# Hybrid RWKV-7 / RG-LRU / MLA layers in float32: the second pair's recurrences issued behind the state chain, another filling for TensorE inside it

## The chip, the cores and the metric

One Trainium2 chip, one NeuronCore. The metric is the device time of one execution in microseconds (us), the median of three runs of one program. The kernel is one launch with no collectives; its inputs lie in the chip's HBM, laid out on the host beforehand.

## The reference

Two layers over 512 tokens of width 1024, then a final RMS norm. Each layer norms `h`, multiplies it with `w_in` and cuts the product into three mixers, gates each by a silu, and adds `y @ w_out` to `h`:

```python
S = S * w_t[:, :, None, :] - sa[..., None] * b_t[:, :, None, :] + v_t[..., None] * k_t[:, :, None, :]   # RWKV-7, 8 heads of 64
...
xc = conv_b + sum(up[:, j:j + T] * conv_w[j] for j in range(CONV_W))        # RG-LRU, width 512, in 8 blocks of 64
gate_r = jax.nn.sigmoid(xb @ ga_w + ga_b); gate_i = jax.nn.sigmoid(xb @ gx_w + gx_b)
log_a = -LRU_C * gate_r * jax.nn.softplus(-lam); a = jnp.exp(log_a)
bx = jnp.sqrt(-jnp.expm1(2.0 * log_a)) * (gate_i * xc)
h_t = a_t * h_(t-1) + bx_t
...
q = rms_norm(q_lat) @ w_uq; kv = rms_norm(kv_lat) @ w_ukv                    # MLA, causal softmax, 8 heads
...
y = jnp.concatenate([y_a * silu(z_a), y_b * silu(z_b), y_c * silu(z_c)], -1); h = h + y @ w_out[l]
```

## The kernel before

All matrix products are float32 made of three float32r products: each operand is split into a high part H and a low part L (`split`, L209; `weights`, L217), and `mm3` (L232) adds H·H, H·L and L·H in PSUM. A piece of weights is loaded by a DMA of the SP queue into one of three `wr` buffers, ScalarE (ACT) copies its H, and VectorE (DVE) or GpSimd (POOL) subtracts to give L; the counter `wmod` says that every so many pieces go to DVE, the others to POOL.

The work of one layer is written as steps of a letter and a number, in the three strings ORD1 to ORD3 (L61 to L63), run in that order. The program's scheduler then places the instructions on each engine by readiness under its own estimate, keeping the priority of the program's order; on the chip each engine runs its list strictly in order and waits for semaphores. So what stands in front of what in an engine's list is fixed at build time.

The prediction is about ORD3, the stretch around the RWKV state chain, which each layer has once:

- **H0 to H7** (`chunk`, L841) are the eight chunks of 64 tokens. Each is a chain across two engines: sixteen small products of the state (L849, "u" below), two DVE additions into `UV` (L852), sixteen small products (L859, "so"), then two DVE instructions that give the next state: the sum with the old state into `S` (L863) and the product with the decays `PC` (L864). Every second chunk also forms the outputs (L877 from the states, L883 from `UV`, then L885 to L887). All `u` and `so` products use the two banks `ck` in turn.
- **A2, A3** (`lru_a`, L672): for one block of 128 channels the projection (24 TensorE matmuls), two ACT copies (L677, L679), three DVE instructions of the convolution (L681), eight small gate matmuls into two `ps` banks (L687), two sigmoids, a POOL product (L691), a tanh (L693).
- **B0, B1** (`lru_b`, L697): the recurrences of a pair of blocks: exp on ACT, the square on POOL (L702), two DVE instructions (L704, L705), a square root (L709) in another ACT table, a POOL product (L710), the DVE scan (L712), a square (L716, L718), a POOL sum (L719), a DVE product with the gate (L720).
- **g0, g1, g2, g3** (`gate`, L372): the four MLA gates, each a projection of 24 matmuls and a silu.
- **t0 to t7** (`lat_products`, L901): the latents' products, eight pieces of 12 matmuls with 416 columns into all four `acc` banks; **T0** copies the four banks out (L916, on ACT), **T1** norms them.
- **N** is the group norm of the chain's outputs (DVE), **R0** the token sums of the RG-LRU outputs (L379), **Y0** the splits of its outputs (L211).

The matmuls of A, g and t have no tie to the chain and fill TensorE (PE) while the chain is on DVE. There are two `ps` banks, four `acc` banks, three `wr` buffers and four each of `wH` and `wL`.

Of the kernel before, what the change touches and what calls it, by code (L numbers as in the profile page):

```python
# [1 line left out]

# [9 lines left out]
AF = mybir.ActivationFunctionType  # L12
# [4 lines left out]
T = 512  # L17
# [30 lines left out]
def body(ctx, tc, x, wc, wl, wo, w2a2, gagx, wuq, wukv, vec, ln_g, fin_g, cst, out, depth=DEPTH):  # L48
# [11 lines left out]
    BN = (2, 2, 0, 0)  # L60
    ORD1 = "M0 L0 L1 C0 M1 C1 P0 L2 O0 M2 U1 O1 C2 U2 P1 L3 M3 C3 U0 P2 O2"  # L61
    ORD2 = "G0 U3 G1 P3 G2 Z0 Z1 O3 G3 X0 f4 V0 V1 Z2 Q0 Q1 f0 V2 V3 f1 Q2 Q3 J0 f2 J1 K0 f3 W0 K1 W1 f5 W2 W3"
    ORD3 = "B0 H0 H1 A2 H2 H3 A3 H4 H5 H6 H7 B1 N0 g0 g1 t0 t6 t1 t2 t4 t5 t3 t7 T0 R0 Y0 g2 g3 T1"  # L63
    LO = "0ig12uw3yvcm"
    Q1 = "aoooottttaaaooookvvqvkqvkqkqqqqq"
    WA, WB, WC, WD, WF = 1000, 2, 2, 5, 1000

    def tl(tag, shape, dt=F32, bufs=1):
        cnt[0] += 1
# [2 lines left out]
    def g2(shape=(128, 512)):  # L72
        return tl("g2", shape, F32, bufs=11)
# [16 lines left out]
    def ps(shape=(128, 512)):  # L90
        cnt[0] += 1
        return PS.tile(list(shape), F32, tag="ps", name=f"ps_{cnt[0]}", bufs=2)
# [40 lines left out]
    def act(out, in_, func, **kw):  # L133
        st = {AF.Sigmoid: "S", AF.Tanh: "S", AF.Sqrt: "Q"}.get(func, "E")
        if cur[0] != st:
            chained(A.preload_act_table_set(SETS[st]))  # L136
            cur[0] = st
        chained(A.activation(out=out, in_=in_, func=func, **kw))  # L138

    def copy(out, in_, **kw):  # L140
        i = A.activation(out=out, in_=in_, func=AF.Copy, **kw)  # L141
        return getattr(i, "ins", i)
# [178 lines left out]
    def one_layer(l):  # L321
        def vc(n, j):
            o = VO[n] + j
            return vecs[:, l, o:o + 1]
# [6 lines left out]
        def proj(j, halves=False):  # L331

            if halves:
                o = acc()
                W = [weights(wc[l, j, :, 4 * hf:4 * hf + 4, :].rearrange("p k c -> p (k c)"), raw=raws.pop((j, hf), None)) for hf in range(2)]
                for th in range(2):
                    t = slice(th * 256, (th + 1) * 256)
                    for k in range(8):
                        s = slice((k % 4) * 128, (k % 4 + 1) * 128)
                        w = W[k // 4]  # L340
                        mm3(o[:, t], (w[0][:, s], w[1][:, s]), (xH[:, k, t], xL[:, k, t]), k == 0, k == 7)
                return o
            o, parts = proj_parts(j)
            for part in parts:
                part()
            return o
# [320 lines left out]
        gw = tl("w2", [128, 2, 4, 64])  # L667
        nc.sync.dma_start(out=gw, in_=gagx[l])

        st = {}  # L670

        def lru_a(*js, o=None):  # L672
            for j in js:
                o = o or proj(17 + j)
                ub = g2([128, T + 3])
                G.memset(ub[:, 0:3], 0.0)
                copy(ub[:, 3:], o)  # L677
                xc = g2()
                A.activation(out=xc, in_=o, func=AF.Identity, scale=vc("cw", 12 + j), bias=vc("cb", j))  # L679
                for t in range(3):  # L680
                    V.scalar_tensor_tensor(out=xc, in0=ub[:, t:t + T], scalar=vc("cw", 4 * t + j), in1=xc, op0=ALU.mult, op1=ALU.add)  # L681
                gt = []
                for w in range(2):
                    o = ps()
                    for e in range(2):
                        hr = slice(64 * e, 64 * e + 64)
                        PE.matmul(o[hr, :], gw[hr, w, j, :], xc[hr, :], start=True, stop=True)  # L687
                    s = g2()
                    act(s, o, AF.Sigmoid, bias=vc("gx_b" if w else "ga_b", j))
                    gt.append(s)  # L690
                G.tensor_tensor(out=gt[1], in0=gt[1], in1=xc, op=ALU.mult)  # L691
                th = g2()
                act(th, gt[0], AF.Tanh, scale=sp8[:, l, j:j + 1])  # L693
                st[j] = (gt[0], gt[1], th)
                o = None

        def lru_b(*js):  # L697
            for j in js:
                a, bx, th = st[j]
                act(a, a, AF.Exp, scale=nsp8[:, l, j:j + 1])  # L700
                a2 = g2()
                G.tensor_tensor(out=a2, in0=a, in1=a, op=ALU.mult)  # L702

                V.scalar_tensor_tensor(out=a2, in0=a2, scalar=1.0, in1=th, op0=ALU.add, op1=ALU.mult)  # L704
                V.tensor_scalar(out=a2, in0=a2, scalar1=1.0e-34, scalar2=None, op0=ALU.max)  # L705
                st[j] += (a2,)
            for j in js:
                a, bx, th, a2 = st[j]
                act(a2, a2, AF.Sqrt)  # L709
                G.tensor_tensor(out=bx, in0=bx, in1=a2, op=ALU.mult)  # L710
                hs = th
                V.tensor_tensor_scan(out=hs, data0=a, data1=bx, initial=0.0, op0=ALU.mult, op1=ALU.add)  # L712
                sq = a2
                if j == 0:
                    stb[0] = tl("sqn", [128, T])
                    A.activation(out=stb[0], in_=hs, func=AF.Square)  # L716
                else:
                    A.activation(out=sq, in_=hs, func=AF.Square)  # L718
                    G.tensor_tensor(out=stb[0], in0=stb[0], in1=sq, op=ALU.add)  # L719
                V.scalar_tensor_tensor(out=hs, in0=hs, scalar=vc("out_g", j), in1=gz[j], op0=ALU.mult, op1=ALU.mult)  # L720
                yb.append(hs)
# [119 lines left out]
        def chunk(ch):  # L841
            cp, par = ch // 2, ch % 2
            ur = slice(64 * (1 - par), 64 * (1 - par) + 64)
            if ch:
                uo = [ck([128, 4, 64]) for _ in range(2)]
                for p in range(4):
                    for e in range(2):
                        hr = slice(64 * e, 64 * e + 64)
                        PE.matmul(uo[e][ur, p, :], AR[p][hr, 0, ch * 64:(ch + 1) * 64], S[ch][hr, p, :], start=True, stop=True)  # L849
                for e in range(2):  # L850
                    u = UV[ur, :, ch, 64 * e:64 * e + 64]
                    V.tensor_tensor(out=u, in0=uo[e][ur, :, :], in1=u, op=ALU.add)  # L852
            if ch < 7:
                so = ck([128, 4, 64])
                for p in range(4):
                    for e in range(2):
                        hr = slice(64 * e, 64 * e + 64)
                        hc = slice(e * 64, (e + 1) * 64)
                        PE.matmul(so[hr, p, :], BT[p][:, ch, hc], UV[:, p, ch, hc], start=True, stop=True)  # L859
                sn = S[ch + 1] = tl("S", [128, 4, 64], bufs=3)  # L860
                pc = PC[:, :, ch:ch + 1].to_broadcast([128, 4, 64])
                if ch:
                    V.tensor_tensor(out=sn, in0=so, in1=S[ch], op=ALU.add)  # L863
                    V.tensor_tensor(out=sn, in0=sn, in1=pc, op=ALU.mult)  # L864
                else:
                    V.tensor_tensor(out=sn, in0=so, in1=pc, op=ALU.mult)
            if par == 0:
                return
            yt = c2([128, 4, 2, 64])
            sq = c2([128, 4, 2, 64])  # L870
            yo = [ps([128, 4, 64]) for _ in range(2)]

            for p in range(4):
                for e, q in ((0, 0), (1, 1), (0, 1), (1, 0)):
                    hr, uq, c = slice(64 * e, 64 * e + 64), slice(64 * q, 64 * q + 64), 2 * cp + q
                    if c:
                        PE.matmul(yo[e][uq, p, :], AR[p][hr, 1, c * 64:(c + 1) * 64], S[c][hr, p, :], start=p == 0, stop=False)  # L877
            for e in range(2):
                hc = slice(e * 64, (e + 1) * 64)
                for p in range(4):  # L880
                    for q in range(2):
                        uq, c = slice(64 * q, 64 * q + 64), 2 * cp + q
                        PE.matmul(yo[e][uq, p, :], AM[q][:, p * 8 + e * 4 + cp, 64:128], UV[:, p, c, hc], start=c == 0 and p == 0, stop=p == 3)  # L883
            for e in range(2):
                V.tensor_copy(out=yt[:, :, e, :], in_=yo[e])  # L885
                A.activation(out=sq[:, :, e, :], in_=yo[e], func=AF.Square)
            V.tensor_reduce(out=vr[:, cp, :, :], in_=sq, axis=AX.X, op=ALU.add)  # L887
            yts.append(yt)
# [53 lines left out]
        def b_split(_):  # L942
            yb[:] = [ysplit(y) for y in yb]

        steps.update({"H": chunk, "N": lambda _: group_norm(), "A": lru_a, "B": lambda i: lru_b(2 * i, 2 * i + 1), "R": b_sums, "Y": b_split,
                      "t": lat_products, "T": latents, "g": lambda p: gzc.append(gate(25 + p))})
        run(ORD2)
        run(ORD3)
# [278 lines left out]
```

## Time and profile before

| what | value |
|---|---|
| three runs | 848.09, 848.45, 851.1 us; median 848.45 |
| the profiled execution | 847.71 us, of which the span is 845.9 |
| mean granted TensorE clock | 0.984 |
| busy: DVE, ACT, POOL | 538.9, 519.3, 353.3 us |
| DMA | 91.07 MB, 108 GB/s on average |

The span is that of the recorded instructions. A row of the timeline gives the start in us from the span's start, the time from its first to its last end, engine, line, operation, output and inputs, the number of instructions merged, and in brackets the idle time before it and what ended it. Matmuls overlap, so their distance from start to start is the cost of one, not the duration in the row. The first layer's state chain stands at about 209 to 258 us of the span, the second layer's at 622 to 672.

### The profile page before, as it was taken

Reading aid. Unit: us, or ns where it says so; the run is one execution under the profiler, and the core shown is the slowest. Engines: PE = TensorE matmul, PEld = TensorE weight load, DVE = VectorE, ACT = ScalarE, POOL = GpSimd, SP = SyncE. Lnnn points to the kernel's source line nnn. Section 1 sums busy time; section 2 is a strip of 40 time slices with the busy share of each in tenths; the row PEclk is TensorE's granted clock in tenths of the full one; section 3 lists DMA queues with packets and bytes.
Section 4 is the critical chain, followed back from the end, with each engine's and each line's share of the span. In section 5 each row is a group of like instructions: output and inputs, shape, how many; then the busy total and the mean of one; then the engine's idle time right before and its main releaser. Section 6 shows DMA issues by size and latency. Waiting matters only on the chain. (4 is left out here: it accounts for less than half of the span.)

```text
span 845.9 us, 15219 instructions
## 1 busy us (share of the span) xinstructions
PE 791.7 (94%) x5696; PEld 619.4 (73%) x5696; DVE 538.9 (64%) x1115; ACT 519.3 (61%) x1018; POOL 353.3 (42%) x321
## 2 busy tenths in 40 slices
PE   4999999999879999999989999999998799999995
PEld 3878888886659877657778788888765697775674
DVE  5678776924977364774474966695367953577636
ACT  5667875657563576664467687845666436765635
POOL 0455557522452455022344556574143425530323
PEclk9999999999998999999999999999999899999998
DMA  7222134311113375123732233332001234731354
GB/s 246 98 76 74 66 111 132 112 58 33 33 39 113 120 229 193 55 90 92 272 122 89 75 100 100 101 112 92 30 26 43 80 95 140 244 120 50 112 174 162
DMA packets 49754, 91.07 MB, mean 108 GB/s; under 512 B 5520, under 2 KB 8336, under 8 KB 49680
## 3 DMA queue, kind: packets, MB, share of 16 engines
q1 hardware_dynamic: 49104, 89.05, 32.8%
q8 instruction: 45, 0.74, 0.4%
q10 hardware_dynamic: 576, 1.05, 0.3%
q14 instruction: 29, 0.24, 0.1%
HBM read 73.30 MB, written 16.78 MB: 106 GB/s over the span
## 5 line engine op out<-in xcount | busy, mean ns | idle before, releaser
L229 POOL TENSOR_TENSOR wL<-wr,wH 128x512 fp32r<-128x512 f32 (+1 forms) x148 | 196.8, 1336 | 283.9 <-ACT wH L141 270.4
L141 ACT ACTIVATE wH<-wr 128x512 fp32r<-128x512 f32 (+1 forms) x192 | 118.8, 622 | 142.8 <-PE acc L234 73.9
L233 PE MATMUL acc<-xH,wH 128*128 128x512 f32 (+1 forms) x496 | 191.9, 388 | 0.0
L234 PE MATMUL acc<-xL,wH 128*128 128x512 f32 (+1 forms) x496 | 189.3, 382 | 0.7 <-DVE xL L306 0.6
L235 PE MATMUL acc<-xH,wL 128*128 128x512 f32 (+1 forms) x496 | 188.5, 380 | 0.0
L234 PEld LDWEIGHTS acc<-xL,wH 128*128 128x128 f32 x496 | 94.0, 190 | 17.5 <-DVE xL L306 1.4
L233 PEld LDWEIGHTS acc<-xH,wH 128*128 128x128 f32 x496 | 93.5, 189 | 18.1 <-ACT xH L141 0.7
L235 PEld LDWEIGHTS acc<-xH,wL 128*128 128x128 f32 x496 | 93.9, 189 | 17.2
L233 PE MATMUL acc<-wH,c 128*128 128x512 f32 x192 | 82.5, 430 | 0.1
L234 PE MATMUL acc<-wL,c 128*128 128x512 f32 x192 | 76.7, 399 | 0.0
L235 PE MATMUL acc<-wH,c 128*128 128x512 f32 x192 | 76.2, 397 | 0.0
L141 ACT ACTIVATE UV<-ps 64x512 f32<-64x512 f32 (+4 forms) x112 | 52.4, 494 | 28.8 <-PE ps L1076 22.0
L229 DVE TENSOR_TENSOR wL<-wr,wH 128x512 fp32r<-128x512 f32 (+1 forms) x44 | 32.6, 744 | 53.0 <-ACT wH L141 52.9
L138 ACT ACTIVATE c<-acc,sm 128x128 f32<-128x128 f32 (+3 forms) x64 | 33.6, 528 | 19.0 <-DVE sm L1060 19.0
L1058 PE MATMUL acc<-am,am 128*128 128x128 f32 (+3 forms) x128 | 42.8, 447 | 0.9 <-ACT c L138 0.8
L234 PEld LDWEIGHTS acc<-wL,c 128*128 128x128 f32 x192 | 36.5, 190 | 8.7 <-issue 1.9
L233 PEld LDWEIGHTS acc<-wH,c 128*128 128x128 f32 x192 | 36.3, 189 | 8.7 <-issue 2.2
L235 PEld LDWEIGHTS acc<-wH,c 128*128 128x128 f32 x192 | 36.3, 189 | 8.2 <-issue 0.5
L136 ACT ACT_TABLE_LOAD x31 | 39.8, 1283 | 1.3 <-PEq L1215 0.7
L138 ACT ACTIVATE g<-g 128x512 f32<-128x512 f32 (+1 forms) x58 | 36.4, 628 | 4.6 <-DVE g L705 2.6
L369 POOL TENSOR_TENSOR g<-g,g 128x512 f32<-128x512 f32 x24 | 32.2, 1340 | 13.9 <-ACT g L138 13.9
L141 ACT ACTIVATE c<-g 128x512 fp32r<-128x512 f32 (+1 forms) x40 | 24.9, 629 | 18.8 <-DVE g L980 7.2
(219 smaller groups left out, 1587.7 us busy)
## 6 DMA issues: line engine op xcount, KB each, us to landing
wr<-in_wc_dram SPq DMA_DIRECT2D x116, 256.0 KB, 2.7
wr<-in_wo_dram SPq DMA_DIRECT2D x48, 256.0 KB, 3.4
hp<-dr SPq DMA_DIRECT2D x38, 256.0 KB, 3.5
dr<-hp SPq DMA_DIRECT2D x28, 256.0 KB, 3.3
dr<-g SPq DMA_DIRECT2D x16, 256.0 KB, 2.5
g<-dr SPq DMA_DIRECT2D x16, 256.0 KB, 3.5
wr<-in_wl_dram SPq DMA_DIRECT2D x16, 208.0 KB, 2.5
dr<-c SPq DMA_DIRECT2D x12, 256.0 KB, 3.7
```

Of the source, the lines that this page charges most:

```text
L136: chained(A.preload_act_table_set(SETS[st]))
L138: chained(A.activation(out=out, in_=in_, func=func, **kw))
L141: i = A.activation(out=out, in_=in_, func=AF.Copy, **kw)
L229: (V if wn[0] % wmod[0] == 0 or wn[0] <= 4 else G).tensor_tensor(out=L, in0=raw, in1=f(H), op=ALU.subtract)
L233: PE.matmul(o, a[0], b[0], start=start, stop=False)
L234: PE.matmul(o, a[0], b[1], start=False, stop=False)
L235: PE.matmul(o, a[1], b[0], start=False, stop=stop)
L369: G.tensor_tensor(out=z, in0=z, in1=s, op=ALU.mult)
L1058: PE.matmul(o[:, 0:n], qT[:, hd, qt * 128:n], K2[:, p, e, 0:n], start=True, stop=True)
```

## The change

In ORD3 the conv, the gates and the recurrences get steps of their own, and the fillings of the chain change places. A `c` step (convolution of a block) is issued on DVE behind the product that ended the last state update before it; an `a` step (gates) has its matmuls behind the last `so` matmul; B1 has its DVE instructions behind the last state update of the whole chain (`tc.issue_after` adds an edge that orders the lists and makes no instruction wait). All eight latents' products stand before g0 and g1. The sum of a state update stays in PSUM, and the square of `a` goes from POOL to ACT.

```diff
-    ORD3 = "B0 H0 H1 A2 H2 H3 A3 H4 H5 H6 H7 B1 N0 g0 g1 t0 t6 t1 t2 t4 t5 t3 t7 T0 R0 Y0 g2 g3 T1"
+    ORD3 = "B0 H0 H1 A2 H2 c2 H3 A3 a2 H4 c3 H5 a3 H6 H7 B1 N0 t0 t6 t1 t2 t4 t5 t3 t7 T0 g0 g1 R0 Y0 g2 g3 T1"
...
+        def lru_in_chain(j):
+            wmod[0] = WE
+            lru_in(j)
+
+        def conv_behind(j):
+            with tc.issue_after(mark["V"]):
+                lru_conv(j)
+
+        def gates_behind(j):
+            with tc.issue_after(mark["P"]):
+                lru_gates(j)
+
+        def lru_b_behind(i):
+            wmod[0] = WE
+            with tc.issue_after(mark["V"]) if i else nullcontext():
+                lru_b(2 * i, 2 * i + 1)
...
                 a2 = g2()
-                G.tensor_tensor(out=a2, in0=a, in1=a, op=ALU.mult)
+                A.activation(out=a2, in_=a, func=AF.Square)
...
-                        PE.matmul(so[hr, p, :], BT[p][:, ch, hc], UV[:, p, ch, hc], start=True, stop=True)
+                        mark["P"] = PE.matmul(so[hr, p, :], BT[p][:, ch, hc], UV[:, p, ch, hc], start=True, stop=True).ins
...
                 if ch:
-                    V.tensor_tensor(out=sn, in0=so, in1=S[ch], op=ALU.add)
-                    V.tensor_tensor(out=sn, in0=sn, in1=pc, op=ALU.mult)
-                else:
-                    V.tensor_tensor(out=sn, in0=so, in1=pc, op=ALU.mult)
+
+                    V.tensor_tensor(out=so, in0=so, in1=S[ch], op=ALU.add)
+                mark["V"] = V.tensor_tensor(out=sn, in0=so, in1=pc, op=ALU.mult).ins
...
-        steps.update({"H": chunk, "N": lambda _: group_norm(), "A": lru_a, "B": lambda i: lru_b(2 * i, 2 * i + 1), "R": b_sums, "Y": b_split,
+        steps.update({"H": chunk, "N": lambda _: group_norm(), "A": lru_in_chain, "c": conv_behind, "a": gates_behind, "B": lru_b_behind, "R": b_sums, "Y": b_split,
```

`lru_in`, `lru_conv` and `lru_gates` are the three parts of `lru_a`, unchanged; `WE` is 2, as `wmod` was there before. Three places of the first layer show what moves; the second layer's lists read the same there.

DVE at the last state update, before. `S` is the state, `g` the tiles of the RG-LRU pair, `UV` and `ck` the chain's operands, `wL` a split of weights for the latents:

```order
L852 TENSOR_TENSOR UV_319<-ck,UV_319 64x4x64
L712 SCALAR_TENSOR_TENSOR g_423_2357<-g_420_2348,g_422_2354 128x512
L712 SCALAR_TENSOR_TENSOR g_443_2498<-g_440_2490,g_442_2495 128x512
L863 TENSOR_TENSOR S_2601<-ck,S_2539 128x256
L229 TENSOR_TENSOR wL_2809<-wr_2806,wH_2808 128x416
L864 TENSOR_TENSOR S_2601<-S_2601,PC_320 128x256
L720 SCALAR_TENSOR_TENSOR g_423_2357<-g_423_2357,vecs,g_352_1723 128x512
L720 SCALAR_TENSOR_TENSOR g_443_2498<-g_443_2498,vecs,g_367_1818 128x512
L852 TENSOR_TENSOR UV_319<-ck,UV_319 64x4x64 x2
```

The same place now: L891 and L892 are the state update, L879 the additions into `UV`, L731, L732 and L739 are B1's L704, L705 and L712 of before, L911 and L913 the outputs' copies and sums:

```order
L879 TENSOR_TENSOR UV_319<-ck,UV_319 64x4x64 x2
L891 TENSOR_TENSOR ck<-ck,S_2526 128x256
L892 TENSOR_TENSOR S_2601<-ck,PC_320 128x256
L879 TENSOR_TENSOR UV_319<-ck,UV_319 64x4x64 x2
L731 SCALAR_TENSOR_TENSOR g_455_2657<-g_455_2657,g_438_2482 128x512
...
L913 TENSOR_REDUCE vr_1209<-c_452_2615 128x8
...
L739 SCALAR_TENSOR_TENSOR g_438_2482<-g_435_2473,g_437_2479 128x512
L739 SCALAR_TENSOR_TENSOR g_449_2581<-g_446_2573,g_448_2578 128x512
L199 TENSOR_SCALAR vr_457_2680<-vr_457_2680 128x32
L229 TENSOR_TENSOR wL_2832<-wr_2829,wH_2831 128x416
```

The two scans and the two products have left the chain; behind them now stands the last split of the latents' weights (`wL_2832`, for t7).

PE at A2's gates (`ps<-g,w`), before, and below it now. L859 and L886 are the `so` products, L849 and L876 the `u` products, `acc` a projection or the latents:

```order
L235 MATMUL acc_2697<-xH_104,wL_2701 128x512
L233 MATMUL acc_2697<-xH_104,wH_2700 128x512
L687 MATMUL ps_2345<-g_418_2340,w_258_1207 64x512 x2
L687 MATMUL ps_2351<-g_418_2340,w_258_1207 64x512 x2
L859 MATMUL ck<-UV_319,c_150_713 64x64 x2
```

```order
L909 MATMUL ps_2390<-UV_319,am_318 64x64
L693 MATMUL ps_2470<-g_418_2340,w_258_1207 64x512 x2
L233 MATMUL acc_2700<-wH_2705,xH_104 128x416
L693 MATMUL ps_2476<-g_418_2340,w_258_1207 64x512 x2
L876 MATMUL ck<-S_2384,c_109_513 64x64 x2
```

The gates stood in front of chunk 2's `so` products; they stand behind chunk 3's now, in front of chunk 4's `u` products.

ACT around T0, now (`wH` the high parts of weights, `wH_2858` and `wH_2876` g0's, `wH_2901` g1's first; `g<-acc` T0's copies):

```order
L136 ACT_TABLE_LOAD
L745 ACTIVATE g_455_2657<-g_438_2482 128x512
L745 ACTIVATE g_456_2662<-g_449_2581 128x512
L141 ACTIVATE wH_2858<-wr_2856 128x512
L141 ACTIVATE c_515_2965<-g_438_2482 128x512
L141 ACTIVATE c_516_2968<-g_449_2581 128x512
L141 ACTIVATE wH_2876<-wr_2874 128x512
L141 ACTIVATE wH_2901<-wr_2899 128x512
L141 ACTIVATE g_488_2847<-acc_2697 128x416
```

T0's copies free the `acc` banks for g0; B1's squares, its splits and g1's first high part now stand in front of them.

More of the change, by code (lines that the diff above doesn't have):

```diff
@@ L1 @@
-from contextlib import ExitStack
+from contextlib import ExitStack, nullcontext
 import concourse.bass as bass
@@ L62, in body @@
     ORD2 = "G0 U3 G1 P3 G2 Z0 Z1 O3 G3 X0 f4 V0 V1 Z2 Q0 Q1 f0 V2 V3 f1 Q2 Q3 J0 f2 J1 K0 f3 W0 K1 W1 f5 W2 W3"
-    ORD3 = "B0 H0 H1 A2 H2 H3 A3 H4 H5 H6 H7 B1 N0 g0 g1 t0 t6 t1 t2 t4 t5 t3 t7 T0 R0 Y0 g2 g3 T1"
+    ORD3 = "B0 H0 H1 A2 H2 c2 H3 A3 a2 H4 c3 H5 a3 H6 H7 B1 N0 t0 t6 t1 t2 t4 t5 t3 t7 T0 g0 g1 R0 Y0 g2 g3 T1"
     LO = "0ig12uw3yvcm"
     Q1 = "aoooottttaaaooookvvqvkqvkqkqqqqq"
-    WA, WB, WC, WD, WF = 1000, 2, 2, 5, 1000
+    WA, WB, WC, WD, WE, WF = 1000, 2, 2, 5, 2, 1000
     def tl(tag, shape, dt=F32, bufs=1):
@@ L668, in one_layer @@
         nc.sync.dma_start(out=gw, in_=gagx[l])
[L670 to L695, printed above, removed]
@@ new lines, in one_layer, with lru_in, lru_conv @@
+        st, mark = {}, {}
+        def lru_in(j, o=None):
+            o = o or proj(17 + j)
+            ub = g2([128, T + 3])
+            G.memset(ub[:, 0:3], 0.0)
+            copy(ub[:, 3:], o)
+            xc = g2()
+            A.activation(out=xc, in_=o, func=AF.Identity, scale=vc("cw", 12 + j), bias=vc("cb", j))
+            st[j] = ub, xc
+        def lru_conv(j):
+            ub, xc = st[j]
+            for t in range(3):
+                V.scalar_tensor_tensor(out=xc, in0=ub[:, t:t + T], scalar=vc("cw", 4 * t + j), in1=xc, op0=ALU.mult, op1=ALU.add)
@@ new lines, in lru_gates @@
+        def lru_gates(j):
+            xc, gt = st[j][1], []
+            for w in range(2):
+                o = ps()
+                for e in range(2):
+                    hr = slice(64 * e, 64 * e + 64)
+                    PE.matmul(o[hr, :], gw[hr, w, j, :], xc[hr, :], start=True, stop=True)
+                s = g2()
+                act(s, o, AF.Sigmoid, bias=vc("gx_b" if w else "ga_b", j))
+                gt.append(s)
+            G.tensor_tensor(out=gt[1], in0=gt[1], in1=xc, op=ALU.mult)
+            th = g2()
+            act(th, gt[0], AF.Tanh, scale=sp8[:, l, j:j + 1])
+            st[j] = (gt[0], gt[1], th)
@@ new lines, in lru_a @@
+        def lru_a(j, o=None):
+            lru_in(j, o)
+            lru_conv(j)
[5 more added lines that the diff above has]
+            with tc.issue_after(mark["V"]):
+                lru_conv(j)
+        def gates_behind(j):
+            with tc.issue_after(mark["P"]):
+                lru_gates(j)
+        def lru_b_behind(i):
+            wmod[0] = WE
+            with tc.issue_after(mark["V"]) if i else nullcontext():
+                lru_b(2 * i, 2 * i + 1)
```

## The prediction

> **What bounds the kernel now.** I read the page first, then TensorE's waits in the stretch of ORD3 in both layers, then the timeline there engine by engine, and the granted clock by windows.
>
> ```profile
> span 845.9 us, 15219 instructions
> PE 791.7 (94%) x5696; PEld 619.4 (73%) x5696; DVE 538.9 (64%) x1115; ACT 519.3 (61%) x1018; POOL 353.3 (42%) x321
> ```
>
> TensorE carries the span, so only its gaps and its slow spells can be won. The waits view of TensorE, of the first layer from 215.9 to 278 us and of the second from 629.4 to 693 us (line, releaser: us in total, times, longest):
>
> ```profile
> PE ck L849 <- DVE S L864: 4.6, 3, 3.1
> PE ps L883 <- DVE UV L852: 2.2, 3, 1.6
> PE ps L687 <- DVE g L681: 2.1, 1, 2.1
> ```
> ```profile
> PE ck L849 <- DVE S L864: 4.6, 3, 3.1
> PE ps L883 <- DVE UV L852: 2.9, 2, 1.6
> PE ps L687 <- DVE g L681: 2.1, 1, 2.1
> ```
>
> Every gap has DVE behind it: the state's product, the additions into `UV`, A2's convolution. The timeline of TensorE at the ends of this stretch, in the first layer and in the second:
>
> ```profile
> 215.84 0.68 PE L849 MATMUL ck<-S,c 64*64 64x64 f32 x16 [1.24 <-DVE S L864]
> ...
> 217.02 0.40 PE L233 MATMUL acc<-xH,wH 128*128 128x512 f32 x1
> 217.25 0.40 PE L234 MATMUL acc<-xL,wH 128*128 128x512 f32 x1
> ...
> 226.17 0.69 PE L859 MATMUL ck<-UV,c 128*64 128x64 f32 x16
> ...
> 277.43 0.35 PE L234 MATMUL acc<-wL,xH 128*128 128x416 f32 x1
> 277.62 0.35 PE L235 MATMUL acc<-wH,xL 128*128 128x416 f32 x1
> 277.81 0.84 PE L379 MATMUL ck<-ones,sqn 128*128 128x2 f32 x7
> ```
> ```profile
> 629.33 0.68 PE L849 MATMUL ck<-S,c 64*64 64x64 f32 x16 [1.25 <-DVE S L864]
> ...
> 692.96 0.39 PE L379 MATMUL ck<-ones,sqn 128*128 128x2 f32 x3
> ```
>
> From chunk 2's `u` products to the token sums it is 61.97 us in the first layer and 63.63 in the second. The bracketed 1.24 and 1.25 are in the waits above and lie before the stretch; without them the gaps inside are 8.9 − 1.24 = 7.7 and 9.6 − 1.25 = 8.3. The granted clock (the number ahead of the last two) sags after them:
>
> ```profile
> 253.50:260.00 6.50, 6.14 (x83) 5.42 (x84) 5.00 (x10) 2.25 (x5) 1.14 (x1) 0.51 0.51 188
> 638.00:654.00 16.00, 16.00 (x224) 10.40 (x223) 10.75 (x22) 9.35 (x15) 4.40 (x4) 0.89 0.23 56
> 667.50:675.00 7.50, 5.84 (x85) 5.18 (x86) 6.00 (x11) 2.92 (x6) 1.47 (x2) 0.63 0.52 169
> 675.00:692.00 17.00, 17.00 (x89) 16.92 (x88) 8.80 (x20) 5.18 (x10) 5.27 (x5) 0.96 0.34 97
> ```
>
> The first layer loses 6.5 × 0.49 = 3.2, less 0.2 that was idle: 3.0. The second loses 16 × 0.11 = 1.8, then 7.5 × 0.37 = 2.8 less 0.6 idle, then 17 × 0.04 = 0.7: 4.7. What is left is TensorE's own work: 61.97 − 7.7 − 3.0 = 51.3 and 63.63 − 8.3 − 4.7 = 50.6. The layers do the same, so I take 51.0.
>
> **The change part by part.**
>
> *B1 and the convolutions out of the chain.* The DVE rows where the longest gap arose (3.1 us), and four others used here and below:
>
> ```profile
> 218.69 1.21 DVE L712 TENSOR_TENSOR_SCAN g<-g,g 128x512 f32<-128x512 f32 x1
> ...
> 220.47 0.67 DVE L887 TENSOR_REDUCE vr<-c 128x8 f32<-128x512 f32 x1
> ...
> 230.96 0.73 DVE L681 SCALAR_TENSOR_TENSOR g<-g,vecs,g 128x512 f32<-128x512 f32 x1
> ...
> 239.97 1.51 DVE L704 SCALAR_TENSOR_TENSOR g<-g,g 128x512 f32<-128x512 f32 x1 [1.47 <-POOL g L702]
> ...
> 247.16 3.44 DVE L712 TENSOR_TENSOR_SCAN g<-g,g 128x512 f32<-128x512 f32 x2
> ...
> 250.97 1.14 DVE L229 TENSOR_TENSOR wL<-wr,wH 128x416 fp32r<-128x416 f32 x1
> 252.03 1.48 DVE L864 TENSOR_TENSOR S<-S,PC 128x256 f32<-128x256 f32 x1
> ...
> 256.44 1.27 DVE L211 TENSOR_TENSOR c<-g,c 128x512 fp32r<-128x512 f32 x2
> ```
>
> Two scans, a split and a slowed product stood between the chain's two ends. All of B1 goes behind the last update, so the 3.1 goes, and the 1.6 in front of L883 as well (B1's L704, 1.51 long, held `UV` up there). The gates behind `so` end the 2.1 at L687: the convolution is long over by then. With no gap of that length the clock should hold, since the gaps of 1.6 in both layers were followed by none of the sags. So I drop all 7.7 and 8.3 and all 3.0 and 4.7, and charge new waits.
>
> [...]
>
> *State sums in PSUM.* The groups of the chain's DVE instructions (busy us, mean ns):
>
> ```profile
> L852 DVE TENSOR_TENSOR UV<-ck,UV 64x256 f32<-64x256 f32 x28 | 10.7, 414 | 3.2 <-PE ck L849 2.9
> ...
> L864 DVE TENSOR_TENSOR S<-S,PC 128x256 f32<-128x256 f32 x12 | 9.4, 787 | 0.1
> ...
> L863 DVE TENSOR_TENSOR S<-ck,S 128x256 f32<-128x256 f32 x12 | 5.1, 422 | 4.7 <-PE ck L859 4.4 <-PE ps L883 0.2
> ```
>
> The same size takes 422 ns with an operand in PSUM and 787 without. A sum written into PSUM is in none of these rows; between `UV`'s 414 and the 787 of L864 I take 422, the row that it is nearest to in size and operands. The product now reads PSUM: 422 too. That is 0.36 us off each of twelve updates, but where it counted it is in the gaps already dropped; should the sums cost 787, four of them that PE would wait for (chunks 2 and 3 in both layers) are 1.4 more.
>
> [...]
>
> *New waits, by hand.* A matmul of 512 columns is 0.23 us (217.02 to 217.25), one of 416 is 0.19, `u` and `so` 0.6 each. I laid the new lists side by side, in the first layer.
> - Chunk 2's `u` starts 0.3 earlier, at 215.5, with two more matmuls (0.5) done ahead: 51.0 − 0.5 = 50.5 of work.
> - To chunk 3: from the end of `UV` at 217.6, DVE waits 0.6 for POOL, then scan 1.2, split 0.6 (half of L211's 1.27), sum over outputs 0.7, product 0.7 (as a convolution's, the same form and size), state sum 0.4, split 0.65, product 0.4: about 222.8. PE has run out of nine projection and five latents' matmuls at 221.9: **0.9**.
> - In chunk 3 three convolutions and a split stand among the `UV` additions: 0.73 + 0.6 + 0.73 + 0.4 until the first of them, against PE's `u` and outputs of 1.35: **1.1**, and 0.15 at `so`.
> - In chunk 5 the same with two ahead: **0.8**. In chunk 7: **0.25**. Chunks 4 and 6 find PE later than DVE, because the gates stand before their `u`.
>
> That is 3.2. For splits and convolutions held up by POOL, and handovers that this plan leaves out, I add 1.3, a product of POOL's length (next rows); the bounds are 0 and three such, 3.9.
>
> *The end.* B1 now runs while PE works off what is left after chunk 6's gates: `u` 0.6, seven latents' matmuls 1.3, `so` 0.6, six more 1.1, `u` and outputs 2.4, 59 latents' matmuls 11.2: 17.2 us. Queued behind B1 on DVE is t7's split; behind that split, on SP, g1's first load, since it needs the buffer; behind that load, on ACT, T0's copies, for whose banks g0 on PE waits. Durations, ACT, then POOL, then the load's landing:
>
> ```profile
> 236.00 0.71 ACT L138 ACTIVATE g<-g,sp 128x512 f32<-128x512 f32 x1
> 236.73 1.28 ACT L136 ACT_TABLE_LOAD   x1
> 238.02 1.34 ACT L138 ACTIVATE g<-g,nsp 128x512 f32<-128x512 f32 x2
> ...
> 276.34 2.19 ACT L141 ACTIVATE g<-acc 128x416 f32<-128x416 f32 x4
> ```
> ```profile
> 243.21 1.28 POOL L710 TENSOR_TENSOR g<-g,g 128x512 f32<-128x512 f32 x1 [2.28 <-ACT g L138]
> ...
> 249.48 3.75 POOL L719 TENSOR_TENSOR sqn<-sqn,g 128x512 f32<-128x512 f32 x2
> ```
> ```profile
> wr<-in_wc_dram SPq DMA_DIRECT2D x116, 256.0 KB, 2.7
> ```
> ```profile
> L718 ACT ACTIVATE g<-g 128x512 f32<-128x512 f32 x6 | 3.8, 632 | 6.3 <-DVE g L712 6.3
> ```
>
> Sigmoid and tanh 2 × 0.7 = 1.4, table 1.3, exps 1.3, squares 2 × 0.63: 5.3. Then DVE's two products and two maxima with the outputs' copies to 8.0, square roots to 9.1, POOL's products to 11.1, scans to 12.4, t7's split to 13.2, or 15.0 if POOL's sums get in between. t7 needs it at 15.2. The load takes 2.7, the high part 0.6, one copy 0.55: 17.1 to 18.9 against 17.2. g0 waits **0.8** (0 to 1.7).
>
> The square costs ACT 0.63 each, hidden in its idle time, and takes 1.3 each off POOL. Loads, weights and matmuls keep their number. The two gates behind the latents' products are only exchanged with these.
>
> *Sum.* A layer's stretch becomes 50.5 + 3.2 + 1.3 + 0.8 = 55.8. The first layer wins 61.97 + 0.3 − 55.8 = 6.5, the second 63.63 + 0.3 − 55.8 = 8.1, together 14.6. The profiled execution of 847.71 (1.8 outside the span) becomes 833.1; the median lies 0.7 above it: **833.8 us**.
>
> **The rivals.**
> - *Clean chain* (832 and below): nothing held up, no wait at the end, both zero: 2 × 2.1 less, 829.6. For it: POOL has little left to do inside the chain. Against it: the split at 250.97 took 1.14 where half of L211's row is 0.63.
> - *The fill on DVE stays a brake* (over 838): convolutions and splits still ahead of `UV`. POOL's holds at 3.9 and g0's wait at 1.7 make it 2 × 3.5 more: 840.8; with the 1.4 of dear sums in PSUM, 842.2.
> - *Slower: B1 in front of g0.* If B1's steps run in series at the slow rows (the 5.3 ahead, DVE's products 2 × 1.5, square roots 1.3, POOL's products 2.6, scans 3.4, sums 3.75, split 1.1, then load, high part and copy 3.85), T0's first copy comes after 24.3, and PE has been dry for 7.1. That is 6.3 more per layer than my 0.8, 846.4, and such a gap chills the clock as the 3.1 did, 3.0 each: 852.4. The sign turns at 5.1 us of wait per layer, the clock's loss counted (14.6 / 2 = 4.3 + 3.0). Against it: the three engines overlap from block to block.
> - *No effect*: the lists change but DVE's work per chunk still bounds the chain, and TensorE waits for it at other lines for as long: 848.45 less the 0.3 of each layer, 847.9. Against it: B1's scans and products leave the chain, and 11 us of latents and as much of g0 and g1 (48 × 0.23) hide them.
>
> **How the numbers follow.** Forecast 0.58, clean chain 0.13, brake 0.18, no effect 0.07, slower 0.04. The range leaves out the last two and the fringe: 829.5 to 842. Half a per cent, 4.2 us, is about what a measurement tells from no change: faster by more 0.88, same 0.08, slower 0.04.
>
> **What would show it.** Right: no TensorE gap over 1.6 us between chunk 2 and the token sums, granted clock 1.00 through it, the state's product at 0.42 us, stretches near 56 us in both layers. Wrong: a gap at g0's first matmul behind ACT's copies, or at t7 behind its split (the end was too cheap); gaps of 2 us in front of the outputs in chunks 3 and 5 (convolutions); a sag at the same place in the second layer without a gap.

## The result, and the profile after

The changed kernel takes 842.49 us (median of four runs, 841.30 to 843.05) against 848.52 for the kernel before on the same chip: ratio 0.9915, 95% interval 0.9899 to 0.9931. It is 6.0 us faster, beyond the half per cent, and 8.7 us above the forecast of 833.8. The profiled execution took 841.3 us; its page:

```profile
span 839.5 us, 15212 instructions
PE 791.0 (94%) x5696; PEld 617.2 (74%) x5696; DVE 540.0 (64%) x1115; ACT 522.0 (62%) x1026; POOL 343.1 (41%) x313
```

TensorE's waits in the first layer's stretch, from chunk 2's `u` to behind the token sums (line, releaser: us in total, times, longest):

```profile
PE acc L233 <- ACT g L141: 3.7, 1, 3.7
PE ck L876 <- DVE S L892: 1.7, 1, 1.7
PE ps L909 <- DVE UV L879: 0.2, 1, 0.2
```

The three long gaps of before (3.1, 2.1, 1.6) are gone. What is left in the chain is 2.0 us, 1.7 of it in front of chunk 3's `u`. In their place stands one gap of 3.7, no longer behind DVE: ACT's copies release g0's first matmul. TensorE's timeline at the ends of the stretch, first layer, then second:

```profile
216.17 0.51 PE L876 MATMUL ck<-S,c 64*64 64x64 f32 x10
...
262.75 0.79 PE L233 MATMUL acc<-xH,wH 128*128 128x512 f32 x1 [3.73 <-ACT g L141]
...
276.24 0.95 PE L379 MATMUL ck<-ones,sqn 128*128 128x2 f32 x8
...
627.43 0.51 PE L876 MATMUL ck<-S,c 64*64 64x64 f32 x10 [0.15 <-DVE S L892]
...
673.99 0.65 PE L233 MATMUL acc<-xH,wH 128*128 128x512 f32 x1 [3.70 <-ACT g L141]
...
686.59 0.95 PE L379 MATMUL ck<-ones,sqn 128*128 128x2 f32 x8
```

The stretches are 60.07 and 59.16 us, where they were 61.97 and 63.63: 6.4 less together, which is the whole difference of the two profiled executions (847.71 to 841.3). The windows (granted clock ahead of the last two numbers):

```profile
208.00:258.50 50.50, 48.27 (x599) 38.13 (x598) 39.82 (x70) 31.13 (x51) 18.12 (x16) 1.00 0.18 53
...
262.70:266.00 3.30, 3.25 (x8) 2.58 (x9) 3.23 (x6) 1.73 (x4) 1.36 (x1) 0.50 0.42 137
266.00:270.00 4.00, 4.00 (x15) 3.17 (x14) 3.98 (x20) 0.63 (x1) 1.40 (x1) 0.75 0.13 30
...
618.00:670.00 52.00, 49.77 (x619) 39.36 (x615) 40.95 (x72) 32.38 (x52) 18.96 (x17) 1.00 0.16 48
...
674.00:678.00 4.00, 4.00 (x11) 3.14 (x12) 3.93 (x8) 1.68 (x4) 1.42 (x1) 0.57 0.44 131
```

The clock holds through both chains and falls behind the new gap: 3.3 × 0.50 + 4 × 0.25 = 2.6 us lost in the first layer, 4 × 0.43 = 1.7 in the second. A layer is now 50.5 (TensorE's own work as the forecast has it) + 2.0 (chain waits) + 3.7 (g0) + 2.6 or 1.7 (clock) + a rest of 1.2.

The chain's two DVE instructions (busy us, mean ns) are as cheap as the forecast had them, 0.42 and 0.43:

```profile
L892 DVE TENSOR_TENSOR S<-ck,PC 128x256 f32<-128x256 f32 x14 | 5.9, 419 | 2.2 <-PE ck L886 2.1
L891 DVE TENSOR_TENSOR ck<-ck,S 128x256 f32<-128x256 f32 x12 | 5.2, 433 | 8.3 <-PE ck L886 8.2
```

Where do T0's copies wait? ACT's, DVE's and POOL's timelines ahead of the gap:

```profile
259.96 1.29 ACT L141 ACTIVATE c<-g 128x512 fp32r<-128x512 f32 x2 [3.81 <-DVE g L747]
261.16 1.13 ACT L141 ACTIVATE wH<-wr 128x512 fp32r<-128x512 f32 x2
262.20 1.72 ACT L141 ACTIVATE g<-acc 128x416 f32<-128x416 f32 x4
```
```profile
251.49 1.22 DVE L198 TENSOR_SCALAR vr<-vr 128x32 int32<-128x32 int32 x1
252.63 2.33 DVE L739 TENSOR_TENSOR_SCAN g<-g,g 128x512 f32<-128x512 f32 x2
...
257.82 1.22 DVE L202 SCALAR_TENSOR_TENSOR vr<-vr,vr 128x32 f32<-128x32 f32 x1
...
259.18 1.41 DVE L747 SCALAR_TENSOR_TENSOR g<-g,vecs,g 128x512 f32<-128x512 f32 x2
```
```profile
254.59 3.15 POOL L746 TENSOR_TENSOR sqn<-sqn,g 128x512 f32<-128x512 f32 x2 [1.91 <-ACT g L745]
257.69 1.29 POOL L229 TENSOR_TENSOR wL<-wr,wH 128x512 fp32r<-128x512 f32 x1
```

TensorE needs the banks at 259.0. T0's copies (`g<-acc`) start at 262.20, since ACT stands 3.81 us in front of Y0's last two split copies, which need L747. L747 could run behind the scans, which end at 254.96. But DVE's list has t7's split and four small instructions of the group norm (`vr`) between them and L747, and three of the four took 1.2 or 1.3 us beside POOL's sums and split.

### The profile page after: what moved, and what is told of

It reads as the page before. It is cut to its first block, busy times and chain, and to the rows that moved or that the text cites. A ratio compares the mean times of both kernels' runs of the same rounds, so it can differ in the third digit from the quotient of the medians.

```text
span 839.5 us, 15212 instructions
## 1 busy us (share of the span) xinstructions
PE 791.0 (94%) x5696; PEld 617.2 (74%) x5696; DVE 540.0 (64%) x1115; ACT 522.0 (62%) x1026; POOL 343.1 (41%) x313
## 5 line engine op out<-in xcount | busy, mean ns | idle before, releaser
L229 POOL TENSOR_TENSOR wL<-wr,wH 128x512 fp32r<-128x512 f32 (+1 forms) x148 | 198.8, 1349 | 272.2 <-ACT wH L141 258.5
L233 PEld LDWEIGHTS acc<-xH,wH 128*128 128x128 f32 x496 | 95.2, 192 | 26.4 <-ACT g L141 8.1
L697 POOL TENSOR_TENSOR g<-g,g 128x512 f32<-128x512 f32 x8 | 10.3, 1282 | 62.6 <-ACT g L138 62.6
```

Source lines behind the costliest of these rows:

```text
L229: (V if wn[0] % wmod[0] == 0 or wn[0] <= 4 else G).tensor_tensor(out=L, in0=raw, in1=f(H), op=ALU.subtract)
L233: PE.matmul(o, a[0], b[0], start=start, stop=False)
```

## The experiments

Theory A: the missing gain lies at g0, because T0's copies stand on ACT behind those split copies; the clock's sag follows. Rival B: the path that the forecast priced, g1's weight load behind t7's split. Rival C: the exchange of g0 and g1 with the latents does more than change places, so that undoing it costs. Rival D: what is won at g0 is lost again behind it. All kernels are the changed one with the edit shown; ratios are to the kernel before, run beside each. The runs stand on several chips, so differences of medians are good to one or two us; where it matters, the difference by the ratios (times 849 us) stands in brackets behind it.

| run | median us | ratio, 95% interval | g0's wait |
|---|---|---|---|
| e9 | 841.15 | 0.9908, 0.9887 to 0.9930 | 3.2 |
| e3 | 839.10 | 0.9880, 0.9863 to 0.9897 | 2.9 |
| e7 | 839.71 | 0.9901, 0.9869 to 0.9934 | none |
| e4 | 852.44 | 1.0052, 1.0033 to 1.0071 | none |
| e12 | 843.23 | 0.9921, 0.9903 to 0.9940 | 3.7 |
| e11 | 837.10 | 0.9849, 0.9827 to 0.9870 | none |
| e14 | 830.91 | 0.9790, 0.9767 to 0.9812 | none |
| e5 | 845.51 | 0.9956, 0.9938 to 0.9974 | 0, 1.4 |
| e6 | 842.46 | 0.9904, 0.9885 to 0.9924 | 0.8, 1.5 |
| e18 | 842.62 | 0.9920, 0.9896 to 0.9944 | none |
| e19 | 843.53 | 0.9923, 0.9903 to 0.9943 | none |
| e20 | 836.87 | 0.9841, 0.9822 to 0.9860 | 1.0, 1.1 |

### e9: g1's weights behind T0's copies

```diff
+                    mark["T"] = copy(ln_t[tt][:, 0:LAT], lat[tt])
...
+            with tc.issue_after(mark["T"]) if p == 1 else nullcontext():
+                gzc.append(gate(25 + p))
```

> g1's weights are put behind T0's copies on ScalarE, nothing else moves. Theory A: T0's copies still stand behind Y0's split copies, so they come earlier only by one high part of 0.57 us: g0's wait 3.1 to 3.2, time 841 to 842.5. Theory B (T0's copies wait for g1's load): g0's wait falls to 0.6 us, the sag goes, time 832 to 834.

g0's wait fell from 3.7 to 3.2, one high part's length, as A has it; the time, 841.15, is not told apart from the changed kernel's by the intervals. B falls: without g1 in front, the copies still wait.

### e3: the group norm behind L747 on DVE

`mark["B"]` is the last L747.

```diff
+        def norm_behind(_):
+            with tc.issue_after(mark["B"]):
+                group_norm()
```

> Only VectorE's list changes: the group norm's small instructions stand behind the second pair's two products L747 instead of ahead of them. Theory A (the changed kernel loses its gain at g0 because T0's copies stand on ScalarE behind Y0's split copies, which wait for L747, which stands behind the group norm's held instructions): L747 starts near 256.6 instead of 259.2 in the first layer, T0's first copy near 260 instead of 262.2, g0's wait falls from 3.7 to 0.8 to 1.7 us per layer, the clock's sag behind it (2.6 and 1.7 us) is gone or halved, time 832 to 837 against 842.5. Theory B (the wait is for g1's weight load and its high part, behind t7's split): no change, 842 to 843, g0's wait stays 3.7.

The time fell by 3.4 us, against B, but g0's wait only to 2.9, where A expected 0.8 to 1.7. TensorE's and DVE's rows:

```profile
262.11 0.69 PE L233 MATMUL acc<-xH,wH 128*128 128x512 f32 x1 [2.94 <-ACT g L141]
```
```profile
256.48 3.47 DVE L747 SCALAR_TENSOR_TENSOR g<-g,vecs,g 128x512 f32<-128x512 f32 x2
...
260.08 0.18 DVE L198 TENSOR_SCALAR vr<-vr 128x32 int32<-128x32 int32 x1
```

L747 started 2.7 us earlier, as expected, and then took 3.47 for two instead of 1.41: it had moved beside POOL's sums and split, where three of the small instructions had taken 1.2 or 1.3 us until then. L198 now took 0.18, while POOL was idle (259.41 to 261.73), where it had taken 1.22. So the order was part of it, and the time lost beside POOL went to whatever stood there; by what means POOL slows DVE no row shows.

### e7: splits and g1 behind T0's copies, the group norm behind L747

```diff
+            first = [ysplit(y) for y in yb[:2]]
+            with tc.issue_after(mark["T"]):
+                yb[:] = first + [ysplit(y) for y in yb[2:]]
```

> Y0's last two split copies and g1's weights behind T0's copies on ScalarE, and the group norm behind L747 on VectorE. Theory A: T0's first copy follows the last latents' product at once, g0's wait 0.6 us (one copy of 0.55) in each layer, no sag behind it, time 831 to 834, which is what the forecast's sum would have given without the wait. Theory B gives the same here; if g0's wait falls and the time stays above 839, the gain was not lost at g0 but somewhere the gap only shows (theory D).

(The edit also holds those of e9 and e3.) g0's wait on ACT is gone altogether, and yet the time is 839.7. The first layer's waits and the cause on DVE:

```profile
PE acc L235 <- DVE wL L229: 2.9, 2, 2.2
```
```profile
270.42 0.68 DVE L229 TENSOR_TENSOR wL<-wr,wH 128x512 fp32r<-128x512 f32 x1
```

The low parts of the second halves of g0's and g1's weights (0.74 and 2.19 us) wait on DVE behind the group norm, its scales and the latents' rotations, and behind the 2.19 the clock fell to 0.75 from 270 to 275 us. That is D's case, if with the same queue as its cause.

### e12: the two gates' low parts on POOL, alone

```diff
+            wmod[0] = 1000 if p < 2 else WC
+            gzc.append(gate(25 + p))
```

> The control of e11: only the low parts of g0's and g1's weights move to GpSimd, ScalarE's list stays. Theory A: T0's copies stand where they stood, g0's wait is 3.7 us as before (3.4 to 4.2, VectorE's list loses 0.7 us ahead of nothing that T0's copies need), time 841.5 to 843.5. If it falls below 838, it is VectorE's load and not the order on ScalarE that made the wait.

As A has it: g0's wait 3.7, time 843.2. Taking these low parts off DVE does nothing for the copies on ACT.

### e11: splits and g1 behind T0's copies, the two gates' low parts on POOL

The splits of e7 together with this; the group norm is where the change has it.

```diff
+            wmod[0] = 1000 if p < 2 else WC
+            with tc.issue_after(mark["T"]) if p == 1 else nullcontext():
+                gzc.append(gate(25 + p))
```

> Built on the changed kernel: Y0's last two split copies and g1's high parts stand behind T0's copies on ScalarE (as in the run e7), and the low parts of g0's and g1's weights are all made by GpSimd, so that none stands on VectorE behind the group norm and the rotations (the 2.9 us that took g0's place in e7); the group norm stays where the change has it. Theory A: no TensorE wait between chunk 3 and the token sums, no sag of the clock there, 3.7 + 2.6 and 3.7 + 1.7 us less than the changed kernel: 830.8, within 829.5 to 833. Theory D (what is won at the gates is lost behind them, since VectorE and ScalarE stay as busy): the waits move behind the token sums, 837 or more. GpSimd's queue as the new bound would show as waits for a low part on GpSimd of 1 us or more.

No wait from chunk 3's outputs to the token sums in either layer, clock 1.00 there. But 837.1, as D has it: the next low part on DVE, g2's second, was late.

```profile
275.64 0.50 PE L235 MATMUL acc<-xH,wL 128*128 128x512 f32 x1 [2.10 <-DVE wL L229]
```
```profile
265.56 4.70 DVE L921 TENSOR_TENSOR c<-c,vr 128x512 f32<-128x512 f32 x4
```

The group norm's four scales took 4.70 beside a gate's product and a split on POOL; in the changed kernel, where POOL stood still, they took 2.50.

### e14: the low parts of all four gates on POOL

```diff
+            wmod[0] = 1000
+            with tc.issue_after(mark["T"]) if p == 1 else nullcontext():
+                gzc.append(gate(25 + p))
+            wmod[0] = WC
```

> As the run e11, but the low parts of all four MLA gates' weights are made by GpSimd: in e11 g0's wait was gone (0 against 3.7 us) and the next one stood at g2's second low part on VectorE, 2.1 us per layer, behind the group norm's scales and the rotations. Theory A: that wait goes too, and the clock's sag behind it in the second layer; time 837.1 - 4.2 - 1.7 = 831, within 830 to 834, the forecast's own range. Theory D (whatever is won is lost again at the next place): a wait of 2 us or more behind g2, at g3 or in the latents' transposes, 836 to 838.

830.91 us, where 831 was expected. Its waits in the first layer's stretch, TensorE's timeline at the ends in both layers, a window, and the page's busy times:

```profile
PE ck L876 <- DVE S L892: 1.9, 2, 1.7
PE ps L909 <- DVE UV L879: 0.2, 1, 0.2
```
```profile
216.80 0.51 PE L876 MATMUL ck<-S,c 64*64 64x64 f32 x10 [0.16 <-DVE S L892]
...
270.42 0.95 PE L379 MATMUL ck<-ones,sqn 128*128 128x2 f32 x8
...
622.46 0.51 PE L876 MATMUL ck<-S,c 64*64 64x64 f32 x10 [0.16 <-DVE S L892]
...
676.02 0.95 PE L379 MATMUL ck<-ones,sqn 128*128 128x2 f32 x8
```
```profile
226.00:270.40 44.40, 44.05 (x471) 36.13 (x461) 37.35 (x57) 25.13 (x42) 21.25 (x16) 1.00 0.32 96
```
```profile
PE 787.0 (95%) x5696; PEld 615.1 (74%) x5696; DVE 558.6 (67%) x1107; ACT 522.0 (63%) x1026; POOL 353.3 (43%) x321
```

The stretches are 53.62 and 53.56 us, 6.5 and 5.6 less than in the changed kernel. DVE is busy 18.6 us longer than there, POOL 10.2, and the time is 11.6 shorter (10.6): what cost was whose turn it was, not how much the engines had to do. Of the 12.1 us won in the stretches 10.4 show in the profiled executions: chunk 2's `u` starts 0.6 later in the first layer (216.80 against 216.17), and from the first stretch's end to the second's start it is 352.0 us instead of 351.2. Why is open.

### e4: the gates ahead of the latents' products, as before

```diff
-    ... H6 H7 B1 N0 t0 t6 t1 t2 t4 t5 t3 t7 T0 g0 g1 R0 Y0 ...
+    ... H6 H7 B1 N0 g0 g1 t0 t6 t1 t2 t4 t5 t3 t7 T0 R0 Y0 ...
```

> The two gates g0 and g1 stand ahead of the latents' products again, as before the change; all else of the change stays. Theory A: no wait at g0's first matmul, T0's copies are wanted by no matmul soon, no sag, time 831 to 835, unless the lack of the latents as cover reopens waits in the chain (each microsecond of wait per layer is 2 us). Theory C (the exchange was needed because the gates are too short a cover or T0 comes too late for what follows): new waits of 3 us or more per layer behind g2 or in the transposes of the latents, time 840 or more.

There is no wait at g0, but at 852.4 the kernel is slower than before. The first layer's waits:

```profile
PE acc L234 <- DVE wL L229: 5.5, 1, 5.5
PE ps L909 <- DVE UV L879: 2.2, 2, 1.4
PE acc L233 <- ACT g L141: 2.0, 1, 2.0
PE ck L876 <- DVE S L892: 1.3, 2, 1.2
```

The latents' second low part waits on DVE behind the group norm and L747, 5.5 us. So A was wrong to add up the wait at g0 as if nothing else hung on the order, and C holds: without the exchange the latents' splits stand behind B1 and the group norm, and with the rest of the change in place the exchange is worth 852.4 − 842.5 = 10 us (11.6).

### e5 and e6: the sums back in SBUF; the square back on POOL

```diff
-                    V.tensor_tensor(out=so, in0=so, in1=S[ch], op=ALU.add)
+                    V.tensor_tensor(out=sn, in0=so, in1=S[ch], op=ALU.add)
...
-                A.activation(out=a2, in_=a, func=AF.Square)
+                G.tensor_tensor(out=a2, in0=a, in1=a, op=ALU.mult)
```

> The state's sums are back in the state's own buffer, all else of the change stays. If the sums in PSUM carry part of the gain (the forecast's term): the state's product goes from 0.42 back to some 0.79 us with the longest near 1.5, the chain's waits rise from 2.0 to 3 to 5 us per layer, time 844 to 848. If they carry none (rival: the update stands behind other work on VectorE anyway): waits 2.0, time within 1 us of 842.5.

> The square of a is back on GpSimd, all else stays. If the square on ScalarE matters (it takes 2 x 1.3 us off GpSimd in the second pair's block, which lies ahead of Y0's split copies): the second pair's scans and L747 come 1 to 3 us later, g0's wait is 4.5 to 6 us instead of 3.7, time 844 to 848. If it is hidden (as the forecast had it): within 1 us of 842.5.

e5: 3.0 us slower. The product takes 564 ns in the mean instead of 419 (some 790 was expected), and chunk 3's wait grows:

```profile
L891 DVE TENSOR_TENSOR S<-S,PC 128x256 f32<-128x256 f32 x12 | 6.8, 564 | 0.1
```
```profile
PE acc L234 <- DVE wL L229: 2.6, 1, 2.6
PE ck L876 <- DVE S L891: 2.5, 2, 2.3
```

The edit reorders DVE's list elsewhere too (the latents' low part waits 2.6, g0 less), so the 3.0 is not the price of the sums alone. Nor is an operand in PSUM the faster one. The product of the kernel before, with both inputs in SBUF (shortest, median and longest in ns):

```profile
L864 DVE TENSOR_TENSOR S<-S,PC x12: 412/613/1478, 215.4 to 666.4; 128x256 f32<-128x256 f32 x12
```

Its shortest, 412 ns, is no longer than the form with PSUM, which takes 411 to 425 in the changed kernel. In e5 ten of the twelve with both inputs in SBUF take 0.41 to 0.43 us, and the two of chunk 2's update, beside a split on POOL, 1.28. The mean of 787 that the forecast set against 422 holds such waits, as in the 1.48 at 252.03, beside POOL's L719 (249.48 to 253.23). In the changed kernel the product with its input in PSUM took 0.42 beside POOL too, and the sum 0.43 (234.50 and 234.03, POOL's split 233.88 to 234.97). What the sums in PSUM take away is these waits.

e6: no change in time, but not because the square was hidden: the waits have other places, 2.6 in front of the outputs, 2.1 at `u`, 1.1 at a low part, 0.8 and 1.5 at g0. TensorE's waits listed here add up to more in the first layer (6.6 us against 5.6), and the mean clock is higher (0.993 against 0.989). What is settled is only the time of it all.

### e18 and e19: the second pair back in the chain

```diff
-    ... H1 A2 H2 c2 H3 A3 a2 H4 c3 H5 a3 H6 ...
+    ... H1 A2 c2 a2 H2 H3 A3 c3 a3 H4 H5 H6 ...
...
-            with tc.issue_after(mark["V"]):
+            with nullcontext():
                 lru_conv(j)
```

(The gates and B1 are freed in the same way. e19 adds the edits of e14.)

> The second pair's inputs, convolutions, gates and recurrences are back at their places in the chain, with nothing held behind the state's update; the state's sums in PSUM, the square on ScalarE and g0 and g1 behind the latents' products stay as changed. If the delay behind the chain is what pays (the forecast): the chain's waits return, 5 to 8 us per layer instead of 2.0 (8.9 before, less what the sums in PSUM save), L747 comes early, so that g0's wait is 0 to 1; with the clock's sag of before, time 843 to 849. Rival (the sums and the exchange of the gates carry the gain, and the delay only moves the wait to g0): waits of 3 to 4 us, time 836 to 841, faster than the changed kernel.

> The run e18 (second pair back in the chain) with the repair of e14 behind the chain (split copies and g1 behind T0's copies, the four gates' low parts on GpSimd). It prices the delay itself, with the end repaired on both sides. If the delay pays what its gaps say: e18's gaps 3.2, 2.2 and 0.4 and their sag stay, nothing was waiting at its gates, so 839 to 843, 8 to 12 us behind e14's 830.9. Rival (the repair alone brings e14's gain, the delay nothing): 831 to 834.

e18's waits in the first layer and two windows, one of each layer:

```profile
PE ps L909 <- DVE UV L879: 3.4, 2, 3.2
PE ps L693 <- DVE g L685: 2.2, 1, 2.2
```
```profile
240.00:260.00 20.00, 16.83 (x202) 14.92 (x203) 18.08 (x31) 10.87 (x19) 8.77 (x6) 0.83 0.28 93
...
660.00:670.00 10.00, 6.84 (x89) 6.35 (x88) 10.00 (x13) 5.42 (x9) 6.50 (x5) 0.69 0.47 154
```

The chain's gaps (6.2 us) and their sag are back, nothing waits at g0, and the time is that of the changed kernel within half a us. So the delay behind the chain, as it was made, won nothing: it exchanged gaps of 3.2 and 2.2 in the chain for one of 3.7 at g0 and one of 1.7. The 6 us of the change are thus what the sums in PSUM, the square and the exchange of the gates give together; no run parts them without the delay. On the repaired end the delay is worth 843.5 − 830.9 = 12.6 us (11.3), the repair alone nothing (842.6 to 843.5), both together 11.7 (11.0).

### e20: all split copies behind T0's copies

On top of e14:

```diff
-            first = [ysplit(y) for y in yb[:2]]
             with tc.issue_after(mark["T"]):
-                yb[:] = first + [ysplit(y) for y in yb[2:]]
+                yb[:] = [ysplit(y) for y in yb]
```

> e14 with the first pair's split copies moved behind T0's copies too, which takes one 1.1 us low part from between the two instructions of chunk 2's state update on VectorE. If chunk 3's wait is what stands ahead of the state's product: 1.7 falls to 0.7, twice 1.0 less, 829. Against it, by theory A: in this order a square root (L745) that waits for the second pair's last scan, which now stands behind the group norm on VectorE, comes ahead of T0's copies on ScalarE; if that is late, g0's wait comes back with 1 to 4 us per layer and the time is 832 to 840, with the cause the same and the instruction in front another.

Chunk 3's wait fell by 0.5, where 1.0 was expected, and g0's came back with 1.0 us: on ACT L745 stands in front of T0's copies and waits for the last scan. (L745 is the square of the scan's output, not a square root as the expectation calls it.) DVE has that scan behind part of the group norm, but it began at 257.07, 0.2 us after POOL's product that it needs ended (256.89), so in the first layer the group norm cost it no more than that.

```profile
258.32 0.63 ACT L745 ACTIVATE g<-g 128x512 f32<-128x512 f32 x1 [0.94 <-DVE g L739]
...
259.38 1.72 ACT L141 ACTIVATE g<-acc 128x416 f32<-128x416 f32 x4
```

The 6.0 us (4.3) that e20 loses on e14 are in part a sag in the second layer, told below. e14 stays the fastest version, 11.6 us (10.6) below the changed kernel and 2.1% below the one before.

## Why the prediction was wrong

- *The end (0.8 per layer)* is the step that failed, and it failed in the path, not in a size. The forecast followed T0's copies back to g1's load and t7's split. The list that it had laid out showed the split copies in front of T0's copies too, but the sum did not follow these to L747 and through the group norm on DVE. Measured: 3.7 per layer. That gap is the first of the forecast's own signs of being wrong. e9 rules out the priced path, e3 moves the wait by DVE's order, e7 and e11 remove it by ACT's.
- *The clock should hold.* It did in the chain, as forecast: 1.00 in both layers, and the 1.8 us sag of the second layer went with its gap. But the new gap chilled it again, 2.6 and 1.7 us. Together with g0 that is 2 × 2.9 + 4.3 = 10.2 us too little; less the 2 × 1.2 of the next point it is 7.8 of the 8.2 by which the profiled execution lies above its forecast of 833.1. The late start adds 0.7 (chunk 2's `u` began at 216.17 in the first layer, not at 215.5), and the handovers take 0.2 back.
- *The chain's waits (3.2)* were too dear: 2.0, all but 0.24 of it in front of chunk 3's `u` (forecast 0.9, measured 1.74); the 1.1 and 0.8 by the convolutions did not come. Chunk 3's is larger because L747 took 1.60 and the split L211 1.10 there, beside POOL, where 0.7 and 0.65 were laid out.
- *Handovers (1.3)*: the rest of the stretches is 1.1 to 1.3 in the changed kernel and in e14, near the forecast. No run shows the term by itself: it is what remains when 50.5 is taken as work, and what DVE lost beside POOL, which the term was meant to cover, shows in chunk 3's wait instead (1.60 and 1.10 above); so that the size fits is partly luck.
- *Sums in PSUM (0.42 us)*: right in duration (0.42 and 0.43). That an operand in PSUM is in itself the faster one the runs do not bear out: without it ten of the twelve products of e5 take 0.41 to 0.43, and only the two beside POOL's split 1.28. e5 shows that they matter, not by how much alone.
- *The exchange of the gates ("only exchanged")*: priced at nothing, and worth 10 us by e4. The time was not wrong by it, as the exchange was made; the reasoning was.
- *The square on ACT (hidden)*: the time is the same without it, but the waits are not; no proof either way.
- *The rivals.* "B1 in front of g0" had the right place with too dear a price (7.1 us against 3.7), and the queue was longer than B1: the group norm stood in it as well. "Clean chain" is near what e14 shows once the end is free: 53.6 us per layer, where it has 50.5 + 3.2 = 53.7, though made of 2.0 of waits and 1.2 of rest. "Brake" with dear sums comes closest to the measured time (842.2), by luck: it holds convolutions up in front of the outputs, and there only 0.24 us is lost.

How long a gap the clock bears the forecast took from the gaps of before (1.6 without a sag, 3.1 with one). Now the 3.73 was followed by a clock of 0.50 over 3.3 us, the 2.94 of e3 by 0.55 over 3.5 us; shorter gaps are told below.

## What to carry to other kernels

When work is moved behind a chain, the next user of that engine's queue is the work's new victim (here T0's copies on ACT, behind Y0's splits: 3.7 us per layer): follow every instruction that stands in front of a releasing copy to what it waits for, on each engine in turn, not only the one that seems last. A wait that is removed shows the next one in the same queue (g0, then the low parts, then g2), so a repair is judged when the last of them is gone. Two edits can each be worth nothing alone and 11 to 12 us together.

## What was not expected of the hardware

The clock's sag can't be read from the length of a gap alone. In e20 TensorE waits almost the same 1.2 us in front of chunk 3's `u` in both layers; in the first the clock stays at 1.00, in the second the next 8 us ran at 0.60:

```profile
223.94 0.51 PE L876 MATMUL ck<-S,c 64*64 64x64 f32 x10 [1.25 <-DVE S L892]
...
631.65 0.51 PE L876 MATMUL ck<-S,c 64*64 64x64 f32 x10 [1.21 <-DVE S L892]
```
```profile
632.00:640.00 8.00, 7.37 (x98) 4.82 (x94) 5.04 (x11) 0.77 (x2) 0.00 (x0) 0.60 0.21 53
```

In e14 a longer gap at that place (1.74 in both layers) had none: 1.00 up to the token sums. The second layer's gap at the second pair's gates is 2.26 us in e18 and 2.24 in e19. In e18 the clock stayed at 1.00 (to 660 us) and the gates' eight matmuls took 1.93 us, in e19 the same eight took 3.10. The longer gaps were followed by sags: 3.13 and 3.11 by 0.51 and 0.63 (before), 3.73 and 3.70 by 0.50 and 0.57 (the changed kernel), 2.94 and 2.93 by 0.55 and 0.72 (e3), 5.54 and 5.04 by 0.73 and 0.86 (e4); those of 3.2 in e18 lie in its windows of 0.83 and 0.69. What else decides it stays open.

Instructions of 128 x 32 elements took up to 1.28 us beside POOL (L201 at 256.51 in the changed kernel) and 0.18 without it (L198: 1.22 in the changed kernel, 0.18 in e3). That is longer than a 128 x 512 one without POOL took (L747 at 216.37 in the changed kernel: 0.74): for this small work on DVE the neighbour on POOL weighed more than the size.
